# A delta-rule stage whose TensorE order is written by hand: projections ahead of time between the scan's matmuls, the next head's preparation inside the scan

## The chip, the cores and the metric

The kernel runs on one core of a Trainium2 chip. The metric is the device time of one execution in microseconds (us). TensorE (PE in the rows) multiplies matrices, VectorE (DVE), ScalarE (ACT) and GpSimd (POOL) do elementwise work, SyncE (SP) issues the DMA transfers between the chip's main memory and its on-chip memory. Each engine takes its instructions in one fixed order; an instruction waits for its operands, and everything behind it on its engine waits with it. So the order in which a kernel's instructions stand on each engine is part of the program.

## What is computed

One layer with two groups of heads that read the same normalised input through one projection. Group A, eight heads, is a gated delta rule, run once in each direction over chunks of 64 tokens (256 context tokens, then 512 latent tokens):

```
a      = strict_lower(k_beta @ k.T * decay)            # per chunk
t_inv  = solve(eye + a, eye)
u, w   = t_inv @ (v * b), t_inv @ (k_beta * exp(g))
def step(s, chunk):                                    # one chunk after the other
    v_new = u - w @ s
    o     = (q * exp(g)) @ s + intra @ v_new
    s     = s * exp(g_last) + (k * exp(g_last - g)).T @ v_new
```

q, k and v of a head are columns of `h @ w_in`, through a convolution over five tokens and a SiLU. Group B is attention with eight query heads and two key/value heads; its q, k and v are other columns of the same product. Both groups are gated by further columns (z) and go through one output projection. All of it is in float32; the large products are made of three products of a high and a low part each.

## The kernel before, in words

**Projections.** One projection tile makes 128 columns of `h @ w_in` for all tokens: 16 steps over the 2048 inputs, in each three matmuls (high x high, low x high, high x low part; L158) of 512 latent columns, and for k, v and the kv tiles three more of 256 context columns (L160). A k, v or kv tile thus streams 36,864 columns, a q or qa tile 24,576. The weights come by SyncE in four pieces a tile (`wraw`), ScalarE casts the high part (`whi`, L122), VectorE or GpSimd makes the low part (`wlo`, L123). The results stand in the accumulators `pl` (512 columns) and `pc` (256 columns, one buffer), from which ScalarE copies them to a buffer `craw`.

**A head of the delta rule** has three parts. *Post*: VectorE does convolution and SiLU of k, q and v (`gdn_post_k`, `gdn_post_q`, `gdn_post_v`). *Preparation* (`gdn_prep`): transposes to tokens (`t1`, `t2`, `t3`, `tv`), the Gram products q k and k k (`gq` L552, `gc` L557), then the inverse of the triangular blocks. Their 16 x 16 corners go through the main memory to `NE` in another layout, 28 small VectorE operations (L603, L605) solve them, they go back through the memory to `DD`, and TensorE combines the blocks in four groups of tiny matmuls on 32 x 32 tiles (`pxa` L626, `pxb` L632, `pxy` L652 and L662) into `UU`. *Scan* (`gdn_scan`): 12 steps, 4 for the context and 8 for the latent tokens, each doing both directions. A step's chain is: ks (L694, L695: state times k) and, on latent steps, the state times q into `o` (L698, L700); r on VectorE (L703); tr = UU times r (L705); vn on ScalarE (L707); su, two state updates of half the array each (L712), and vn into `o` (L722); the new state st on VectorE (L718, twice). After the last step a head's output is normalised (`on`), transposed (`ot`, L735), scaled by ScalarE (`oc`) and stored to `o_d` (L738).

**The order.** In program order a head's projections stand first, then its preparation, then its scan; after head 7 come four kv tiles and three qa tiles, stored to `kvd` and `qad` for the attention. A scheduler orders all five engines by its own model of times; in this stage nothing is ordered by hand, except that the gates of heads 1 to 7 are issued after a marked instruction of head 0's preparation. So the projections of later heads, the kv and the qa tiles fill TensorE between the scan's matmuls wherever the scheduler put them. The attention, from the transposes of the first kv head on (`kps0`, L877), has a TensorE order written by hand. Its loads are norm weights (`nw`), rotary tables (`rope`, of which VectorE makes `tabk`), the mixer inputs `M` from `o_d`, queries `qc` from `qad` and `kvch` from `kvd`.

Stages in the profiled execution: the input stage and head 0's projections to about 161 us, the delta-rule stage to 860, attention to 1233, output projection to the end.

Of the kernel before, what the change touches and what calls it, by code (L numbers as in the profile page):

```python
# [68 lines left out]
def build(tc, a):  # L69
# [77 lines left out]
    def proj_steps(col, nm, pl, pc=None):  # L147

        for kq in range(4):
            src = w_in[kq * 512:(kq + 1) * 512, col:col + 128].rearrange("(k p) c -> p k c", p=128)  # L150
            hi, lo = wpiece(src, f"{nm}_{kq}", 128)
            for k4 in range(4):
# [8 lines left out]
                yield  # L161
# [177 lines left out]
    for j in range(3):  # L339
        V.tensor_copy(gsb[:, 256 * j:256 * j + 256], gps[32 * j:32 * j + 32])  # L340
    gso = p1a.tile([32, 6, 2, 64], F32, name="gso")
    for lo_c, n in ((0, 4), (4, 8)):
        v = gsb[:, lo_c * 64:(lo_c + n) * 64].rearrange("p (c t) -> p c t", t=64)
        p_lo = 0 if n == 4 else 2
        V.tensor_copy(gso[:, p_lo:p_lo + n // 2, 0], v[:, 0:n // 2])
        V.tensor_copy(gso[:, p_lo:p_lo + n // 2, 1], v[:, n // 2:n][:, ::-1])
    gtp = gtile([128, 6, 32], "gtp")
    for p in range(6):
        T.transpose(out=gtp[:, p], in_=gso[:, p].rearrange("g h t -> g (h t)"), identity=ident[:32, :32])
# [8 lines left out]
    for hf_ in range(2):  # L358
        pr = slice(64 * hf_, 64 * hf_ + 64)
        for v in range(2):  # L360
            d = v if hf_ == 0 else 1 - v
            src = gtp[pr].rearrange("t p (k d h) -> t d k h p", k=2, d=2)[:, d]
            V.tensor_copy(gx[pr, :, :, v], src)
            s2 = adt[pr].rearrange("t k (d h) -> t d k h", d=2)[:, d].unsqueeze(3).to_broadcast([64, 2, 8, 6])
            V.tensor_copy(adv[pr, :, :, v], s2)
# [4 lines left out]
    S.activation(gsc["beta"], flat(gx[:, 0]), AF.Tanh, scale=0.5)  # L370
    V.tensor_scalar(out=gsc["beta"], in0=gsc["beta"], scalar1=0.5, scalar2=0.5, op0=ALU.mult, op1=ALU.add)
# [6 lines left out]
    V.tensor_tensor(out=zg, in0=flat(gx[:, 1]), in1=flat(adv[:, 1]), op=ALU.add)  # L378
    V.tensor_copy(ag, flat(adv[:, 0]))
    V.scalar_tensor_tensor(out=ug, in0=zg, scalar=-1.0, in1=zg, op0=ALU.mult, op1=ALU.min)  # L380
    for q_ in range(0, 96, 12):
        G.tensor_tensor(out=ug[:, q_:q_ + 12], in0=ep[:, q_:q_ + 12], in1=ug[:, q_:q_ + 12], op=ALU.pow)
    es1a.close()

    def gates(h0, h1):
# [18 lines left out]
        gcp = gtile([128, 2, n], "gcp" + nm)  # L404
        gtot = [gtile([128, n], f"gtot{i}" + nm) for i in range(2)]
        gcv = gcp.rearrange("p s (h v q) -> p s h v q", v=2, q=6)
# [12 lines left out]
        V.tensor_scalar(out=gsc["negeg"][:, cols], in0=gsc["negeg"][:, cols], scalar1=-1.0, scalar2=None, op0=ALU.mult)  # L419
        gtr = gtile([n, 128], "gtr" + nm)  # L420
# [7 lines left out]

    gates(0, 1)
# [19 lines left out]

    def gdn_post_k(h, pl, pc):  # L450
        kq = qkp.tile([128, 8, 128], F32, tag="kq", bufs=3, name=f"kq{h}")
        kc = qkp.tile([128, 2, 2, 64], F32, tag="kc", bufs=2, name=f"kc{h}")
# [7 lines left out]
        return kq, kc  # L460

    def gdn_post_q(h, kq, pl):
# [5 lines left out]
    def gdn_post_v(h, pl, pc):  # L468
        vv = qkp.tile([128, 6, 2, 64], F32, tag="vv", bufs=1, name=f"vv{h}")
# [5 lines left out]
        return vv  # L475

    mark = [None]

    def gdn_prep(h, kq, kc, vv):

        nm = f"h{h}"
        UU, IB = UUs[h % 2], IBs[h % 2]
# [11 lines left out]
        for p in range(4):  # L494
            S.activation(jk, t1[:, p], AF.Square, accum_out=ss[:, p:p + 1])
        for p in range(4):
            T.transpose(out=t2[:, p], in_=kq[:, 7 - p], identity=ident)
        S.copy(ktok[64:128, 2:6], t2[64:128])
        for p in range(4):
            S.activation(jk, t2[:, p], AF.Square, accum_out=ss[:, 4 + p:5 + p])  # L500
        t3 = gtile([128, 2, 128], f"t3{nm}")
# [45 lines left out]

        gq = gtile([128, 4, 2, 64], f"gq{nm}")
        for p in range(4):
            for s, c in ((0, p), (1, 7 - p)):  # L550
                kv = kq[:, c].rearrange("p (s t) -> p s t", s=2)
                T.matmul(gq[64 * s:64 * s + 64, p], lhsT=kv[:, s], rhs=kv if s == 0 else kv[:, ::-1],  # L552
                         start=True, stop=True, skip_group_check=True)
        gc = gtile([128, 2, 64], f"gc{nm}")
        for p in range(2):
            for s in range(2):
                T.matmul(gc[64 * s:64 * s + 64, p], lhsT=kc[:, p, s], rhs=kc[:, p, s],  # L557
# [9 lines left out]
        for v in range(2):  # L567
            mul(V, grv[:, v, 2:6], gq[:, :, 0], grv[:, v, 2:6])
            mul(V, grv[:, v, 0:2], gc, grv[:, v, 0:2])
# [7 lines left out]

        vtok = gp.tile([128, 6, 128], F32, tag="vtok", bufs=2, name=f"vtok{nm}")
        for p0_, n in ((0, 2), (2, 4)):
            tv_ = gtile([128, n, 128], f"tv{nm}_{p0_}")  # L580
            for p in range(n):
                T.transpose(out=tv_[:, p], in_=vv[:, p0_ + p].rearrange("c s t -> c (s t)"), identity=ident)
            for p in range(n):
                S.activation(vtok[:, p0_ + p], tv_[:, p], AF.Copy, scale=vin[:, p0_ + p:p0_ + p + 1])
# [12 lines left out]
        mark[0] = V.memset(NE.rearrange("w j i -> w (j i)")[:, 0:256:17], 1.0).ins  # L597
# [12 lines left out]

# [591 lines left out]
```

## Time and profile before

| | |
|---|---|
| median of 3 runs | 1435.78 us (1430.89 to 1436.18) |
| the profiled execution's own time | 1433.8 us |
| its span, first to last instruction | 1432.0 us |
| mean granted TensorE clock | 0.986 |
| TensorE, VectorE, GpSimd, ScalarE busy | 1316.3, 733.7, 500.1, 494.2 us |

Busy time says which engine has the most work, not where the end is set. For that the span is cut into stages, and in each one reads how long TensorE stood and what ended its waits. A wait is printed as "engine, instruction <- what ended it: us in total, times, longest". In the names, h is a head's number left out, `bk` is the bank that holds ks, tr and one of the su, and "64*128" is the part of the array that a matmul uses.

### The profile page before, as it was taken

Reading aid. Unit: us, or ns where it says so; the run is one execution under the profiler, and the core shown is the slowest. Engines: PE = TensorE matmul, PEld = TensorE weight load, DVE = VectorE, ACT = ScalarE, POOL = GpSimd, SP = SyncE. Lnnn points to the kernel's source line nnn. Section 1 sums busy time; section 2 is a strip of 40 time slices with the busy share of each in tenths; the row PEclk is TensorE's granted clock in tenths of the full one; section 3 lists DMA queues with packets and bytes.
Section 4 is the critical chain, followed back from the end, with each engine's and each line's share of the span. In section 5 each row is a group of like instructions: output and inputs, shape, how many; then the busy total and the mean of one; then the engine's idle time right before and its main releaser. Section 6 shows DMA issues by size and latency. Waiting matters only on the chain. (4 is left out here: it accounts for less than half of the span.)

```text
span 1432.0 us, 25185 instructions
## 1 busy us (share of the span) xinstructions
PE 1316.3 (92%) x9710; PEld 1011.0 (71%) x9710; DVE 733.7 (51%) x1618; ACT 494.2 (35%) x1212; POOL 500.1 (35%) x473
## 2 busy tenths in 40 slices
PE   3898899999999999999899996999999999998997
PEld 1455678666677777777677785777787877776785
DVE  3443686757456575656362135535648456533222
ACT  4111354243243433343232223444334433533221
POOL 1011554443424343333323244333343333333530
PEclk9999999999999999999999998999999999999999
DMA  9999444232313131413122277223425243464202
GB/s 308 279 295 283 121 100 101 47 73 43 83 38 96 37 95 31 98 43 82 35 58 62 55 224 223 68 67 104 131 70 160 74 130 103 160 235 139 89 35 98
DMA packets 278708, 163.58 MB, mean 114 GB/s; under 512 B 79868, under 2 KB 252501, under 8 KB 277565
## 3 DMA queue, kind: packets, MB, share of 16 engines
q1 hardware_dynamic: 278589, 161.98, 41.3%
q8 instruction: 76, 1.25, 0.4%
q14 instruction: 43, 0.35, 0.1%
HBM read 150.43 MB, written 11.51 MB: 113 GB/s over the span
## 5 line engine op out<-in xcount | busy, mean ns | idle before, releaser
L123 POOL TENSOR_TENSOR wlo_z<-wraw_z,whi_z 128x512 fp32r<-128x512 f32 x64 | 86.0, 1344 | 152.8 <-ACT whi_z L122 152.8
L686 POOL TENSOR_SCALAR keh<-ktokh,esuf 128x128 f32<-128x128 f32 x88 | 55.3, 629 | 169.7 <-PE bkh L712 169.6
L158 PE MATMUL zl<-hhL,whi_z 128*128 128x512 f32 x256 | 108.4, 423 | 0.0
L158 PE MATMUL zl<-hlL,whi_z 128*128 128x512 f32 x256 | 103.1, 403 | 0.0
L158 PE MATMUL zl<-hhL,wlo_z 128*128 128x512 f32 x256 | 102.9, 402 | 0.0
L707 ACT ACTIVATE vnh<-bkh,cch 128x128 f32<-128x128 f32 x96 | 35.2, 367 | 174.2 <-PE bkh L705 174.1
L140 PE MATMUL po<-wlo_wo,mh 128*128 128x512 f32 x192 | 76.7, 400 | 6.4 <-POOL wlo_wo L123 4.8
L139 PE MATMUL po<-whi_wo,mh 128*128 128x512 f32 x192 | 75.8, 397 | 0.1
L141 PE MATMUL po<-whi_wo,ml 128*128 128x512 f32 x192 | 75.8, 395 | 0.0
L1042 DVE SCALAR_TENSOR_TENSOR gacc<-graw,scol,gacc 128x512 f32<-128x512 f32 x60 | 56.1, 934 | 32.7 <-DMA graw<-in_w_ada 32.2
L123 POOL TENSOR_TENSOR wlo_qa<-wraw_qa,whi_qa 128x512 fp32r<-128x512 f32 x32 | 43.2, 1351 | 73.5 <-ACT whi_qa L122 73.5
L718 DVE SCALAR_TENSOR_TENSOR sth<-sth,egl,suh 128x128 f32<-128x128 f32 x80 | 27.7, 346 | 77.8 <-PE bkh L712 77.2
L123 POOL TENSOR_TENSOR wlo_wo<-wraw_wo,whi_wo 128x512 fp32r<-128x512 f32 x24 | 35.6, 1483 | 82.6 <-ACT whi_wo L122 82.5
L122 ACT CAST whi_z<-wraw_z 128x512 fp32r<-128x512 f32 x64 | 39.6, 621 | 64.8 <-PE zl L158 21.7
L158 PEld LDWEIGHTS zl<-hhL,wlo_z 128*128 128x128 f32 x256 | 49.3, 193 | 11.9
L158 PEld LDWEIGHTS zl<-hlL,whi_z 128*128 128x128 f32 x256 | 49.6, 194 | 8.7
L158 PEld LDWEIGHTS zl<-hhL,whi_z 128*128 128x128 f32 x256 | 49.6, 194 | 8.7
L123 DVE TENSOR_TENSOR wlo_wo<-wraw_wo,whi_wo 128x512 fp32r<-128x512 f32 x24 | 20.0, 838 | 68.7 <-ACT whi_wo L122 66.1
L251 PE MATMUL ada<-wada,cs 128*32 128x256 f32 x512 | 41.9, 414 | 12.6 <-DMA wada<-in_w_ada 12.6
L319 POOL TENSOR_TENSOR wlo<-wraw,whi 128x384 fp32r<-128x384 f32 x16 | 16.0, 1004 | 105.6 <-ACT whi L318 105.6
L123 POOL TENSOR_TENSOR wlo_q<-wraw_q,whi_q 128x512 fp32r<-128x512 f32 x24 | 33.3, 1389 | 54.8 <-ACT whi_q L122 46.6
L703 DVE SCALAR_TENSOR_TENSOR rh<-bkh,negeg,vtokh 128x128 f32<-128x128 f32 x88 | 30.8, 350 | 41.9 <-PE bkh L695 41.4
(387 smaller groups left out, 4099.8 us busy)
## 6 DMA issues: line engine op xcount, KB each, us to landing
wada<-in_w_ada SPq DMA_DIRECT2D x128, 256.0 KB, 5.1
graw<-in_w_ada SPq DMA_DIRECT2D x64, 256.0 KB, 2.7
wraw_z<-in_w_in SPq DMA_DIRECT2D x64, 256.0 KB, 2.8
wraw_wo<-in_w_out SPq DMA_DIRECT2D x48, 256.0 KB, 3.0
wraw_qa<-in_w_in SPq DMA_DIRECT2D x32, 256.0 KB, 2.8
wraw_k<-in_w_in SPq DMA_DIRECT2D x28, 256.0 KB, 2.9
wraw_q<-in_w_in SPq DMA_DIRECT2D x28, 256.0 KB, 2.7
wraw_v<-in_w_in SPq DMA_DIRECT2D x28, 256.0 KB, 2.8
```

The lines of the kernel that those rows point to most:

```text
L122: S.copy(hi, raw)
L123: (lo_eng or G).tensor_tensor(out=lo, in0=raw, in1=hi, op=ALU.subtract)
L139: T.matmul(out, lhsT=lh, rhs=rh, start=start, stop=False, skip_group_check=True)
L140: T.matmul(out, lhsT=lh, rhs=rl, start=False, stop=False, skip_group_check=True)
L141: T.matmul(out, lhsT=ll, rhs=rh, start=False, stop=stop, skip_group_check=True)
L158: T.matmul(pl, lhsT=lw, rhs=rt[0][:, k], start=st, stop=sp, skip_group_check=True)
L251: T.matmul(ada_ps[32 * g:32 * g + 32], lhsT=cs[:, kk], rhs=wt[:, kk % 4].rearrange("p s c -> p (s c)"), start=kk < 4, stop=kk >= KT - 4, s ...
L686: G.tensor_scalar(out=ke, in0=ktok[:, p], scalar1=gsc["esuf"][:, gcol:gcol + 1], scalar2=None, op0=ALU.mult)
L703: V.scalar_tensor_tensor(out=r, in0=ks, scalar=gsc["negeg"][:, gcol:gcol + 1], in1=vtok[:, p], op0=ALU.mult, op1=ALU.add)
L707: S.activation(vn, tr, AF.Copy, scale=cc[:, 0, w:w + 1])
L718: V.scalar_tensor_tensor(out=sn[:, d], in0=st[:, d], scalar=egl[:, half, gcol:gcol + 1], in1=su, op0=ALU.mult, op1=ALU.add)
L1042: V.scalar_tensor_tensor(out=acc, in0=raw, scalar=scol[:, k:k + 1], in1=acc, op0=ALU.mult, op1=ALU.add)
```

## The change

TensorE's order from the end of head 0's projections to the last qa tile is now the program's order (`manual_schedule` for TensorE alone); the other engines are still ordered by the scheduler. The program order is written with generators:

- `feed` runs over the projection tiles in the order q1, k1, v1, kv0, kv1, then k, q, v of heads 2 to 7, then kv2, kv3, qa0, qa1, qa2. `pull(n)` takes steps from it until n columns are streamed.
- `gdn_scan` yields after ks and o (2600 columns are pulled there), after tr (2900) and after su and o (2900): 35 slots a head.
- `gdn_prep` of the next head is cut into 11 pieces. One piece is emitted at each of the slots in `PREP_AT`; `gc` is in the fifth (slot 9), `pxa` in the eighth (slot 24).
- The output transposes of a head (`ot`) are emitted at slot 6 of the next head's scan; those of head 7 after all else.
- VectorE's, ScalarE's and GpSimd's operations of the scan, and those of the gates, get the scheduler's priority `first_of_all` (2500, where the solve's operations have 1500).

Also: `gc` and its use stand behind `gq`'s, and `tv` and `vtok` behind the solve; `kc` has three buffers instead of two, `ke` two instead of three, `r` one instead of two; a kv tile is stored in two transfers; the gates' totals share a bank. The arithmetic and the number of matmuls are the same.

```
+    F1, F2, F3 = 2600, 2900, 2900
+    PREP_AT = (0, 2, 4, 6, 9, 11, 13, 24, 26, 29, 31)
+    def first_of_all():
+        return tc.high_priority(offset=2500)
+    es_p0.enter_context(tc.manual_schedule(engines={mybir.EngineType.PE}))
...
+    def feeding():
+        yield from feed_q(1)
+        yield from feed_k(1)
+        yield from feed_v(1)
+        for i in range(2):
+            yield from feed_kva(i)
+        for h in range(2, NH):
+            yield from feed_k(h)
+            yield from feed_q(h)
+            yield from feed_v(h)
+        for i in range(2, 4):
+            yield from feed_kva(i)
+        for h in range(QSPILL):
+            yield from feed_qa(h)
...
+    def pull(n):
+        debt[0] += n
+        while debt[0] > 0:
+            c = next(feed, None)
+            if c is None:
+                debt[0] = 0
+                return
+            debt[0] -= c
...
+    for n in (3000, 5500, 5500, 4000, 12000, 4000):
+        pull(n)
+        next(prep, None)
+    run(g1, 5000, 9000, 3000)
...
+    run(prep, 4000, 24000, 4000, 5000, 4000)
+    tail = None
+    for h in range(NH):
+        while h + 1 < NH and h + 1 not in fed:
+            pull(1)
+        scan = gdn_scan(h)
+        prep = gdn_prep(h + 1) if h + 1 < NH else iter(())
+        slot = 0
+        for n in scan:
+            if n is None:
+                break
+            pull(n)
+            if slot in PREP_AT:
+                next(prep, None)
+            if slot == 6 and tail is not None:
+                next(tail, None)
+            slot += 1
+        for _ in prep:
+            pull(3000)
+        tail = scan
+    pull(12000)
+    next(tail, None)
+    for _ in feed:
+        pass
```

What this does to the order is shown at three places. First TensorE at the end of the stage. Before, around the output transposes of head 7 (`oth`; `kvl` and `kvx` are the accumulators of tile kv3):

```order
L160 MATMUL kvx_8835<-hlC,whi_kv_0_8838 128x256
L158 MATMUL kvl_8834<-hhL,wlo_kv_0_8839 128x512
L160 MATMUL kvx_8835<-hhC,wlo_kv_0_8839 128x256
L158 MATMUL kvl_8834<-hhL,whi_kv_0_8838 128x512
L160 MATMUL kvx_8835<-hhC,whi_kv_0_8838 128x256
L158 MATMUL kvl_8834<-hlL,whi_kv_0_8838 128x512
L160 MATMUL kvx_8835<-hlC,whi_kv_0_8838 128x256
L158 MATMUL kvl_8834<-hhL,wlo_kv_0_8839 128x512
L735 MATMUL oth_8450<-cmain,onh_8442 128x128 x4
L160 MATMUL kvx_8835<-hhC,wlo_kv_0_8839 128x256
```

After, from the last step of head 7's scan (now L722 to L728 for ks and o, L735 for tr, L755 for vn into o) to the first attention transposes (`kpsh`) and the first z projection:

```order
L722 MATMUL bkh_11_9160<-sth_10_9156,kq_7391 64x128
L723 MATMUL bkh_11_9160<-sth_10_9156,kq_7391 64x128
L726 MATMUL oh_8981<-sth_10_9156,qeh_8076 64x128
L728 MATMUL oh_8981<-sth_10_9156,qeh_8076 64x128
L735 MATMUL bkh_11_9160<-rh_11_9165,UU_2041 128x128
L755 MATMUL oh_8981<-vnh_11_9168,IB_1559 128x128
L770 MATMUL oth_9181<-cmain,onh_9173 128x128 x4
L998 MATMUL kps_9268<-cmain,kvch_9266 128x128 x6
L159 MATMUL zl_9298<-hhL,whi_z_0_9301 128x512
```

The kv and qa tiles that stood around and behind the output transposes are gone from there; in after, the last projection matmul of the feed stands in step 5 of this scan, and steps 6 to 11, oth and kps0 follow one another with no projection between.

Second, SyncE from the store of head 7's output on. Before, from three rows behind that store (`wraw` are weights, `graw` weights of the gate vector):

```order
L816 DMA nw_9230<-in_q_norm_w 128x128
L817 DMA nw_9230<-in_k_norm_w 128x128
L131 DMA wraw_qa1_1_9056<-in_w_in 128x4x128
L785 DMA kvd_8458<-craw0_1530 128x768
L827 DMA ropek0_9237<-in_rope 128x512
L131 DMA wraw_qa1_2_9074<-in_w_in 128x4x128
L827 DMA ropek1_9239<-in_rope 128x512
L1038 DMA graw0_0_10297<-in_w_ada 128x512
L1038 DMA graw0_1_10300<-in_w_ada 128x512
L131 DMA wraw_qa1_3_9092<-in_w_in 128x4x128
L872 DMA kvch00_9261<-kvd_8458 128x768
L872 DMA kvch01_9306<-kvd_8458 128x768
```

After, from the store itself:

```order
L773 DMA o_d_1469<-och7_9172 128x512
L937 DMA nw_9235<-in_q_norm_w 128x128
L938 DMA nw_9235<-in_k_norm_w 128x128
L948 DMA ropek0_9242<-in_rope 128x512
L948 DMA ropek1_9244<-in_rope 128x512
L1172 DMA M0_9207<-o_d_1469 128x512
L1172 DMA M1_9208<-o_d_1469 128x512
L1172 DMA M2_9209<-o_d_1469 128x512
```

Four rows on, behind M3 to M6:

```order
L1172 DMA M7_9214<-o_d_1469 128x512
L1036 DMA qc0_9262<-qad_1563 128x512
L1036 DMA qc1_9264<-qad_1563 128x512
L993 DMA kvch00_9266<-kvd_1562 128x768
L993 DMA kvch01_9311<-kvd_1562 128x768
```

The loads for the attention stand directly behind the store of head 7's output, with the eight M loads ahead of qc and kvch; before, weights of the qa tiles stood between them, and the M loads came later than all of these rows.

Third, TensorE at the first scan matmul of head 0 (L705 before, L735 after). Before (`gq` belongs to the preparation of head 1, `ql` to the projection of head 2):

```order
L158 MATMUL ql_3214<-hhL,wlo_q_1_3236 128x512
L158 MATMUL ql_3214<-hhL,whi_q_1_3235 128x512
L552 MATMUL gqh_2596<-kq_2301 64x128 x3
L705 MATMUL bkh_0_1959<-vtokh_1683,UU_1587 128x128
L552 MATMUL gqh_2596<-kq_2301 64x128 x4
L712 MATMUL suh_0_1963<-vnh_0_1961,keh_0_1957 128x128
L712 MATMUL bkh_0_1959<-vnh_0_1961,keh_0_1957 128x128
L552 MATMUL gqh_2596<-kq_2301 64x128
L158 MATMUL ql_3214<-hlL,whi_q_1_3235 128x512
L158 MATMUL ql_3214<-hhL,wlo_q_1_3236 128x512
```

After (`pxy` belongs to the preparation of head 0, `kvl` and `kvx` to tile kv0, `t1` to the preparation of head 1):

```order
L684 MATMUL pxyh_2306<-DTh_2065,XTh_2287 32x32 x2
L684 MATMUL pxyh_2306<-DDh_2064,XTh_2287 32x32
L735 MATMUL bkh_0_2374<-vtokh_1906,UU_1552 128x128
L159 MATMUL kvl_2152<-hhL,whi_kv_1_2296 128x512
L161 MATMUL kvx_2153<-hhC,whi_kv_1_2296 128x256
L159 MATMUL kvl_2152<-hlL,whi_kv_1_2296 128x512
L161 MATMUL kvx_2153<-hlC,whi_kv_1_2296 128x256
L159 MATMUL kvl_2152<-hhL,wlo_kv_1_2297 128x512
L161 MATMUL kvx_2153<-hhC,wlo_kv_1_2297 128x256
L504 MATMUL t1h_2387<-cmain,kq_1687 128x128 x4
L744 MATMUL suh_0_2398<-vnh_0_2376,keh_0_2372 128x128
L744 MATMUL bkh_0_2374<-vnh_0_2376,keh_0_2372 128x128
```

The scan of head 0 now starts straight behind its own preparation, at a point where the feed has reached kv0; counted over the whole order, about 145,000 projection columns stand ahead of this matmul before and about 114,000 after, and head 2's q and v stand between the scans of head 0 and head 1.

More of the change, by code (lines that the diff above doesn't have):

```diff
@@ L568, in gdn_prep @@
             mul(V, grv[:, v, 2:6], gq[:, :, 0], grv[:, v, 2:6])
+        yield
+        gc = gtile([128, 2, 64], f"gc{nm}")
+        for p in range(2):
+            for s in range(2):
+                T.matmul(gc[64 * s:64 * s + 64, p], lhsT=kc[:, p, s], rhs=kc[:, p, s],
+                         start=True, stop=True, skip_group_check=True)
+        for v in range(2):
             mul(V, grv[:, v, 0:2], gc, grv[:, v, 0:2])
@@ L656, in gdn_prep @@
         V.tensor_copy(XT, pxy[:, 0])
+        yield
         for p in range(6):
@@ new lines, in run @@
+    def run(gen, *pulls):
+        for n in pulls:
+            pull(n)
+            if next(gen, gen) is gen:
+                return
+        for _ in gen:
+            pull(2000)
+    g0, g1 = gates(0, 1), gates(1, NH)
+    pull(1500)
+    with first_of_all():
+        next(g0, None)
+    pull(16000)
+    with first_of_all():
+        next(g0, None)
+    pull(3000)
+    with first_of_all():
+        next(g0, None)
+    prep = gdn_prep(0)
+    for n in (3000, 5500, 5500, 4000, 12000, 4000):
+        pull(n)
+        next(prep, None)
```

239 lines of the change are left out of this document (132 added, 107 removed).

## The prediction

> **What bounds the kernel now.** I read the page first. Its first lines say what the whole span is made of.
>
> ```profile
> span 1432.0 us, 25185 instructions
> PE 1316.3 (92%) x9710; PEld 1011.0 (71%) x9710; DVE 733.7 (51%) x1618; ACT 494.2 (35%) x1212; POOL 500.1 (35%) x473
> ```
>
> TensorE is busy for 92% of the span and no other engine for more than 51%, so the order of TensorE can win at most the time in which TensorE stands, and lose whatever it adds to that. Next I cut the span by stage, with the columns start and end, length, and busy time by engine with the granted clock after POOL's column.
>
> ```profile
> 161.00:251.00 90.00, 82.82 (x730) 67.39 (x729) 67.36 (x179) 42.10 (x117) 48.70 (x35) 0.98 0.38 90
> 251.00:860.00 609.00, 581.53 (x5456) 443.36 (x5453) 327.34 (x853) 205.17 (x568) 224.60 (x247) 0.99 0.29 71
> 860.00:905.00 45.00, 33.74 (x146) 26.91 (x145) 24.71 (x41) 16.33 (x54) 19.94 (x18) 0.81 0.62 189
> ```
>
> The change touches these three stretches: the start (161 to 251, idle 7.2 us), the scans with their fillers (251 to 860, idle 609.0 - 581.5 = 27.5 us) and the entry to attention (860 to 905, idle 11.3 us). The waits of TensorE between 251 and 860 come from another view (total, times, longest), and one row each from the same view for 161 to 251 and for 860 to 905.
>
> ```profile
> PE oth L735 <- DVE onh L732: 7.0, 6, 2.0
> PE pxah L626 <- DVE DTh L619: 4.5, 4, 1.2
> PE pxbh L632 <- issue: 4.2, 4, 1.7
> PE bkh L694 <- DVE sth L718: 2.1, 3, 1.3
> PE oth L735 <- DVE tmh L603: 2.0, 2, 1.0
> PE pxyh L662 <- issue: 1.6, 1, 1.6
> PE ktp L877 <- DVE kn L852: 5.1, 1, 5.1
> ```
>
> No wait is large. The biggest group is the transposes of a head's output (oth), 9.0 us in all; the scan itself (bk) waits for 2.1 us. Last the inside of one scan step, from the timeline of TensorE (start, duration), VectorE and ScalarE, in head 7:
>
> ```profile
> 785.92 0.32 PE L694 MATMUL bkh<-sth,kq 128*64 128x128 f32 x1
> 786.97 0.38 PE L705 MATMUL bkh<-rh,UU 128*128 128x128 f32 x2
> 787.31 0.39 PE L158 MATMUL kvl<-hhL,whi_kv 128*128 128x512 f32 x1
> 787.54 0.28 PE L160 MATMUL kvx<-hhC,whi_kv 128*128 128x256 f32 x1
> 787.97 0.34 PE L712 MATMUL suh<-vnh,keh 64*128 64x128 f32 x1
> 788.95 0.28 PE L160 MATMUL kvx<-hlC,whi_kv 128*128 128x256 f32 x1
> 789.06 0.39 PE L158 MATMUL kvl<-hhL,wlo_kv 128*128 128x512 f32 x1
> 789.38 0.32 PE L694 MATMUL bkh<-sth,kq 128*64 128x128 f32 x1
> 786.41 0.35 DVE L703 SCALAR_TENSOR_TENSOR rh<-bkh,negeg,vtokh 128x128 f32<-128x128 f32 x1 [0.80 <-PE bkh L695]
> 788.46 0.35 DVE L718 SCALAR_TENSOR_TENSOR sth<-sth,egl,suh 128x128 f32<-128x128 f32 x1 [1.70 <-PE bkh L712]
> 788.72 0.34 DVE L718 SCALAR_TENSOR_TENSOR sth<-sth,egl,bkh 128x128 f32<-128x128 f32 x1
> 787.45 0.37 ACT L707 ACTIVATE vnh<-bkh,cch 128x128 f32<-128x128 f32 x1 [2.59 <-PE bkh L705]
> ```
>
> Four numbers come out of this. A 512-column projection matmul occupies TensorE for 787.54 - 787.31 = 0.23 us, so 0.455 ns a column. The same matmul ahead of a small-tile matmul takes 789.38 - 789.06 = 0.32 us, so a change between the full array and a 64-wide tile costs about 0.09 us. The 256 columns at 787.54 need 0.12 us and the change 0.09, yet the state update (su) starts 0.43 us later: 0.2 us of hidden waiting for vn, which no idle row shows. And the whole step takes 3.46 us, with 3072 projection columns in it (1.40 us), so the scan's own matmuls occupy about 1.86 us.
>
> **The change part by part**, against the profiled execution's own time of 1433.8 us (span 1432.0; the median of the runs shown is 1435.8, from 1430.9 to 1436.2, so this execution lies 2 us under the median).
>
> *Array changes.* Counted in the two orders from the gate transposes to the first attention transposes, there are 506 changes between full and small tiles before and 433 after. 73 x 0.094 = 7 us less; nothing hides them, they are TensorE's own time. **-7**; 0 if the shorter streaks drain less.
>
> *The start.* Before the first scan matmul of head 0, before streams about 145,000 projection columns and after about 114,000: 31,000 x 0.455 ns = 14.1 us of work moved behind it. It is a gain only if the scan of head 0 starts 14 us sooner. Its chain is gates, Gram products, the triangular solve on VectorE, and pxa:
>
> ```profile
> 237.22 0.57 DVE L619 STREAM_TRANSPOSE DTh<-DDh 128x384 f32<-128x384 f32 x1
> 240.93 0.22 PE L626 MATMUL pxah<-DTh,grh 32*32 32x32 f32 x2
> 251.30 0.48 PE L705 MATMUL bkh<-vtokh,UU 128*128 128x128 f32 x2
> ```
>
> DT is ready at 237.8 and pxa follows 3.1 us later: by hand that goes. The gates' VectorE work now runs first of all, and nothing else of head 1 is between pxa and the scan; I put 3 us on both, from the 10.4 us that now lie between pxa and the first scan matmul. So the scan starts 6 us sooner for 14.1 us of missing cover: **+8**. Ends: +3 if the chain shrinks by 11 us, +15 if it does not shrink at all and something slips by a microsecond.
>
> *Waits in the scans.* The fixed slots stand 6 or more matmuls of a projection (2304 to 3072 columns, 1.05 to 1.4 us) at each of the three hand-overs of a step. The hand-over from vn to su needs 787.97 - 786.97 = 1.0 us, that to ks 789.38 - 787.97 = 1.4 less its own 0.4, that to tr 1.05. So the scan's waits go, the hidden ones too: 0.2 us in about half of some 90 steps, 10 us, with the visible 27.5 us 37 us together. oth goes to a fixed slot in the next head's scan, long after it is ready; pxb and pxy keep some 6 us, since their waits are for evacuations that are no shorter. What is late next is pxa. One head of before shows its chain:
>
> ```profile
> 493.06 0.45 PE L557 MATMUL gch<-kc 128*64 128x64 f32 x6
> 503.25 0.17 DVE L603 TENSOR_TENSOR tmh<-NEh 96x14 f32<-96x14 f32 x1
> 516.14 0.16 DVE L605 TENSOR_TENSOR NEh<-NEh,tmh 96x14 f32<-96x14 f32 x1
> 526.42 0.22 PE L626 MATMUL pxah<-DTh,grh 32*32 32x32 f32 x2 [1.07 <-DVE DTh L619]
> ```
>
> gch to pxa is 33.4 us; its solve on VectorE took 12.9 us, where 28 operations of about 0.2 us need some 6 with other work between, so I take 31. In the order of after, about 41,500 columns (18.9 us) and five steps (9.3 us) stand between gch and pxa: 28.2 us. So pxa stops TensorE by 0 to 5 us in each of 7 heads; I take 2.5, 17 us. And ten tiles now follow one another on the single context accumulator (v, then k), which must wait for ScalarE's copy; the nearest row is two kv tiles that do so:
>
> ```profile
>   ACT craw L784: 0.6, 2
> L182 ACT COPY craw<-kx x7: 365/374/398, 186.6 to 665.6; 128x256 f32<-128x256 f32 x7
> ```
>
> 0.3 us each, up to 0.8 where a cast is ahead of the copy: 5 us for ten. The spill stores of the kv and qa tiles now pass through SyncE's queue during the scans, ahead of transfers of the solve, and wait there for that same copy; I cost them at nothing, since weights are loaded a tile ahead, and at 0.4 us for each of 7 tiles if not. With 3 us for small slips, these among them, 31 us stay of 37. **-6**, from -26 (pxa never late, no slips) to +12 (5 us a head).
>
> *The end of the stage.* Here the order of after is plain: the feed of projections runs out in step 6 of the last scan. The steps left (5.5) stand bare, then oth of head 7, then kps0 directly. In before, kv3 and three qa tiles, some 100,000 columns or 45 us, stood between. A bare step is its chain, from the rows above: ks to r 0.49, r 0.35, to tr 0.21, to vn 0.48, vn 0.37, to su 0.15, to st 0.49, both st 0.60, together 3.14, with the next ks 3.2 us instead of 1.86 us of own work: 5.5 x 1.34 = +7. The last oh, the transposes and the loads behind them stand in the next rows, with the landing time of the M loads last.
>
> ```profile
> 808.71 0.49 PE L722 MATMUL oh<-vnh,IB 128*128 128x128 f32 x2
> 812.98 0.63 PE L735 MATMUL oth<-cmain,onh 128*128 128x128 f32 x4 [1.09 <-DVE onh L732]
> 815.65 0.46 SPq L738 DMA_DIRECT2D o_d<-och  x1
> 871.60 3.64 SPq L1051 DMA_DIRECT2D M<-o_d  x8
> M<-o_d SPq DMA_DIRECT2D x8, 256.0 KB, 5.1
> 859.88 0.82 PE L877 MATMUL kps<-cmain,kvch 128*128 128x128 f32 x6
> 870.00:880.00 10.00, 3.77 (x15) 2.94 (x16) 5.91 (x9) 3.79 (x11) 4.68 (x4) 0.63 0.90 308
> ```
>
> Last oh to oth is 4.3 us, of which TensorE waited 1.1 and now all: +3. Behind oth, SyncE's queue in after holds the store of o_d, the two norm loads, two rope loads, eight M loads, two qc, and only then kvch, for which kps0 waits. From the rows: oth to the issue of o_d 2.7, o_d with nw and rope issues 2.3 (five at about 0.46), eight M and two qc 4.6, then kvch lands in about 5 behind the 2.5 MB ahead of it, since 3 MB at 308 GB/s last 9.7 us from the first M: 14.7, less oth's own 0.6: 14. Before had all of this under the 45 us of projections (kps0 follows without a wait at 859.88). I take 13, between 6 (kvch bound only by its own issue) and 17. The entry that follows then finds loaded weights and an emptier queue, where ktp waited 5.1 us and the clock fell to 0.63: -4 of its 11.3 us. **+19**, from +9 to +24.
>
> Here a rule speaks against the change. In the row 870 to 880, TensorE is busy for 3.8 of 10 us and its granted clock is 0.63. The Trainium skill, "TensorE: Matmul & The Clock Gate", Part 1: The HAM clock gate, says that a window of about 3.4 us without enough work halves the clock, and that a like window of work restores it; by that, the 13 us wait would end in about 3.4 us at half speed, some 1.7 us more. The drop in the row agrees in direction; no run here shows the window.
>
> Sum: 8 - 7 - 6 + 19 = +14, so 1433.8 + 14 = **1448**.
>
> **The rivals.**
>
> *Faster.* The solve of the next head is done when pxa comes up (31 us becomes 28), and the chain of head 0 is 11 us shorter: +3 - 7 - 26 + 19 = -11, **1423**. For it: the steps between are long, and the scan's VectorE work goes first, so no wait is passed on; the present pxa waits are at most 1.2 us. Against it: pxa comes after a fixed number of columns, not when it is ready.
>
> *No change.* The end costs half, since steps 6 to 11 are partly covered by slips of the feed and kvch is issued before M's bytes fill the engines: loads 6, bare 4, oth 3, entry -4 = +9, and +4 in all, **1438**. For it: SyncE issues a load in 0.46 us, and what is ahead of kvch could be issued while the bare steps run. Against it: SyncE's queue, where all of it stands behind the store of o_d.
>
> *Slower still.* The solve's 28 operations stand in VectorE's queue between the state updates of step 5 and of step 7; if their input lands later than the queue reaches them, the scan stands behind them too. The input came 10.2 us after gch in the rows (493.06 to 503.25); the queue reaches it about 2.3 steps of 5.7 us later, 13 us. If it slips by more than 3 us, each head pays the 3 us more: 7 x 3 = +21, **1469**. It decides from a landing 13 us after gch.
>
> *Clock.* During the bare steps TensorE is busy for 1.86 of 3.2 us. At a clock of 0.63 for 5.5 steps its 10.2 us become 16.2, +6, **1454**. No stretch of the trace has TensorE half busy for so long, so it has little for or against it. The page of the Trainium skill named above speaks of idle and busy windows and does not say where 58% falls.
>
> **How the numbers follow.** Forecast 0.37 (own range 1443 to 1457), faster 0.27 (1416 to 1428), no change 0.20, slower still 0.11, clock 0.05. Half a per cent, 7 us, is about what a measurement of this kernel can tell from no change; faster by more has 0.27, within it 0.20, slower by more 0.37 + 0.11 + 0.05 = 0.53. The range for 8 in 10 goes from 1418, inside the faster case, to 1470, the upper rival.
>
> **What would show it.** Right: in the profile after, the last scan's steps are 3.2 us apart with idle rows behind r and vn, kps0 waits over 10 us for the DMA of kvch, the first scan matmul of head 0 is at 244 to 248, oth has no wait. Wrong: kps0 waits under 5 us (the end is not dear); pxa waits under 5 us in all while head periods fall below those of before (faster); waits of bk for st or r of over 20 us (slower still). A start of head 0's scan before 240 would break the first term.

## The result, and the profile after

The changed kernel takes 1470.0 us (median, 1467.1 to 1470.8) where before takes 1435.1: ratio 1.0245, interval 1.022 to 1.0271. It is slower, as forecast, but by 35 us and not by 14, just outside the range on record (1418 to 1470). The profiled execution took 1469.6, its span 1467.8, 35.8 us over before's span; the sums below are made against that. (Of e2_more_columns two of four executions were disturbed; its time is given by the other two.)

The first lines of the page after:

```profile
span 1467.8 us, 25179 instructions
PE 1310.9 (89%) x9710; PEld 1011.6 (69%) x9710; DVE 725.8 (49%) x1618; ACT 493.4 (34%) x1212; POOL 498.9 (34%) x473
```

TensorE has 5.4 us less to do than before, and stands 41 us longer. Its waits over the whole span, the rows of the changed stage alone:

```profile
PE gcp L414 <- issue: 20.2, 1, 20.2
PE kps L998 <- DMA kvch<-kvd: 15.6, 1, 15.6
...
PE pxah L645 <- DVE DTh L637: 12.4, 6, 4.8
...
PE bkh L722 <- DVE sth L749: 8.3, 6, 1.9
...
PE oth L770 <- DVE onh L766: 3.8, 1, 3.8
...
PE kx L161 <- ACT craw L183: 3.7, 5, 1.1
```

Two single waits stand out, one at the start (gcp, the cumulative gates of head 0) and one at the end (kps0, for kvch). Between the heads little is left: the many waits for oth are gone, and what pxa waits is 12.4 us in all, 4.8 of it in head 0. The windows of the two ends, with the middle between them in the second row (start and end, length, busy time by engine from TensorE on, then granted clock, DMA share and GB/s):

```profile
166.00:192.00 26.00, 5.10 (x22) 3.54 (x20) 13.24 (x39) 4.27 (x9) 20.93 (x10) 0.65 0.16 40
261.00:800.00 539.00, 512.79 (x4869) 400.70 (x4870) 295.27 (x791) 193.10 (x543) 202.80 (x221) 0.99 0.28 66
846.00:875.00 29.00, 25.06 (x138) 16.94 (x136) 6.70 (x21) 4.44 (x10) 6.84 (x8) 0.74 0.15 43
882.00:897.00 15.00, 0.30 (x2) 0.30 (x3) 1.50 (x5) 0.04 (x1) 0.00 (x0) 0.50 0.83 307
```

The middle is dense at a clock of 0.99; at both ends the clock falls, down to 0.50. What holds the start is read from VectorE and GpSimd:

```profile
175.50 0.16 DVE L403 SCALAR_TENSOR_TENSOR ug<-ug,w_g 128x12 f32<-128x12 f32 x1
186.81 1.81 DVE L397 TENSOR_SCALAR s_g<-ug 128x84 f32<-128x84 f32 x1 [11.15 <-POOL ug L386]
191.68 0.17 DVE L407 SCALAR_TENSOR_TENSOR gg__1452<-zg,ag 128x12 f32<-128x12 f32 x1
167.62 19.15 POOL L386 TENSOR_TENSOR ug<-ep,ug 128x12 f32<-128x12 f32 x8 [3.11 <-DVE ug L384]
```

GpSimd raises `ug` to a power in eight pieces, 2.4 us each. Head 0 needs the first piece. The operation on 84 columns is the first gate operation of heads 1 to 7 and needs the seven others; it stands in VectorE's queue ahead of the last seven of head 0's gate operations (those on 12 columns), so these wait 11.15 us with it, and gcp on TensorE behind them. And the end, TensorE's rows from the bare steps (tr of steps 6 to 11) to the attention, and SyncE's:

```profile
855.35 0.49 PE L735 MATMUL bkh<-rh,UU 128*128 128x128 f32 x2 [0.23 <-DVE rh L732]
858.50 0.49 PE L735 MATMUL bkh<-rh,UU 128*128 128x128 f32 x2 [0.23 <-DVE rh L732]
862.09 0.80 PE L735 MATMUL bkh<-rh,UU 128*128 128x128 f32 x2
866.11 0.80 PE L735 MATMUL bkh<-rh,UU 128*128 128x128 f32 x2
870.12 0.79 PE L735 MATMUL bkh<-rh,UU 128*128 128x128 f32 x2
874.13 0.79 PE L735 MATMUL bkh<-rh,UU 128*128 128x128 f32 x2
880.01 1.09 PE L770 MATMUL oth<-cmain,onh 128*128 128x128 f32 x4 [3.78 <-DVE onh L766]
896.70 1.54 PE L998 MATMUL kps<-cmain,kvch 128*128 128x128 f32 x6 [15.60 <-DMA kvch<-kvd]
```

```profile
882.06 0.34 SPq L773 DMA_DIRECT2D o_d<-och  x1
884.43 5.13 SPq L1172 DMA_DIRECT2D M<-o_d  x8
889.94 0.94 SPq L1036 DMA_DIRECT2D qc<-qad  x2
891.25 0.94 SPq L993 DMA_DIRECT2D kvch<-kvd  x2
```

The first two bare steps are 3.15 us apart, the last ones 4.01 us, not 3.2, and their tr takes 0.80 us where it took 0.49 in the first two. Between them the granted clock falls:

```profile
856.00:858.00 2.00, 1.31 (x14) 1.02 (x14) 0.61 (x2) 0.30 (x1) 0.94 (x2) 1.00 0.48 164
858.00:860.00 2.00, 1.16 (x12) 0.74 (x8) 0.35 (x1) 0.37 (x1) 0.00 (x0) 0.94 0.34 99
860.00:862.00 2.00, 2.00 (x13) 1.22 (x10) 0.92 (x3) 0.00 (x0) 0.60 (x1) 0.50 0.00 0
```

### The profile page after: what moved, and what is told of

Its sections match the earlier page's. It is cut to its first block, busy times and chain, and to the rows that moved or that the text cites. A ratio compares the mean times of both kernels' runs of the same rounds, so it can differ in the third digit from the quotient of the medians.

```text
span 1467.8 us, 25179 instructions
## 1 busy us (share of the span) xinstructions
PE 1310.9 (89%) x9710; PEld 1011.6 (69%) x9710; DVE 725.8 (49%) x1618; ACT 493.4 (34%) x1212; POOL 498.9 (34%) x473
## 4 chain that ended last, share of the span: by engine, by line
PE 64%; DVE 12%; DMA 9%; issue 5%; POOL 4%; ACT 3%; SPq 2%; POOLq 0%; DVEq 0%; ACTq 0%
PE zl L159 9%; PE qal L159 5%; PE vl L159 5%; PE kl L159 4%; PE ql L159 4%; PE po L140 3%; PE kvl L159 3%; PE po L141 3%; PE po L139 3%; DMA wada<-in_w_ada 3%; PE vx L161 2%; PE suh L744 2%; DMA graw<-in_w_ada 2%; PE kx L161 2%; PE bkh L722 2%
## 5 line engine op out<-in xcount | busy, mean ns | idle before, releaser
L712 POOL TENSOR_SCALAR keh<-ktokh,esuf 128x128 f32<-128x128 f32 x88 | 61.4, 698 | 66.0 <-PE bkh L744 65.2
L751 DVE SCALAR_TENSOR_TENSOR sth<-sth,egl,suh 128x128 f32<-128x128 f32 x80 | 27.5, 344 | 84.8 <-PE bkh L744 82.0
L1163 DVE SCALAR_TENSOR_TENSOR gacc<-graw,scol,gacc 128x512 f32<-128x512 f32 x60 | 53.0, 884 | 19.5 <-DMA graw<-in_w_ada 19.2
L159 PE MATMUL qal<-hhL,whi_qa 128*128 128x512 f32 x128 | 54.1, 423 | 0.0
L159 PE MATMUL kl<-hhL,whi_k 128*128 128x512 f32 x112 | 52.7, 470 | 0.0
```

The costliest lines, as they stand in the source:

```text
L159: T.matmul(pl, lhsT=lw, rhs=rt[0][:, k], start=st, stop=sp, skip_group_check=True)
L712: G.tensor_scalar(out=ke, in0=ktok[:, p], scalar1=gsc["esuf"][:, gcol:gcol + 1], scalar2=None, op0=ALU.mult)
L1163: V.scalar_tensor_tensor(out=acc, in0=raw, scalar=scol[:, k:k + 1], in1=acc, op0=ALU.mult, op1=ALU.add)
```

## The experiments

Twelve kernels, each compared with before on the chip that it ran on. "The start" is the time of head 0's first scan matmul (251.3 before, 261.1 after).

**e1_gates_behind: the mark put back.**

```
-        V.memset(NE.rearrange("w j i -> w (j i)")[:, 0:256:17], 1.0)
+        mark[0] = V.memset(NE.rearrange("w j i -> w (j i)")[:, 0:256:17], 1.0).ins
...
+            with tc.issue_after(mark[0]):
+                done = next(gen, gen) is gen
...
-    g0, g1 = gates(0, 1), gates(1, NH)
+    g0, g1 = gates(0, 1), behind_mark(gates(1, NH))
```

> The changed kernel with one thing put back: VectorE's gate operations of heads 1 to 7 are again issued behind head 0's NE memset. Theory 1 (the start was lost in VectorE's queue): the operation on 84 columns that waited 11.15 us for GpSimd's power operations no longer stands in front of head 0's gates, so gcp comes at 179 to 182 us instead of 191.9, TensorE's wait there is 8 to 10 us instead of 20.2, the first scan matmul of head 0 comes at 249 to 252 instead of 261.1, and the time falls from 1470 by 10 to 12 to about 1459. Rival (TensorE's own order is the loss: gcp stands too early in it, and the chain behind is as long anyway): the first scan matmul stays after 257 and the time falls by less than 4.

1457.5 us, ratio 1.0173 (1.0144 to 1.0201), 12.6 less than after. gcp came at 178.2, the start at 251.1. Its waits of TensorE between 161 and 251:

```profile
PE gcp L414 <- issue: 8.4, 1, 8.4
PE gcp L414 <- DVE gg__1452 L407: 8.2, 1, 8.2
```

The mark is worth about 12 us (12.6 by the medians, 10 by the two ratios, whose intervals are 4 us to either side), and theory 1 holds for that part. It isn't the whole: the start is back where before has it, but TensorE still stands 16.6 us on the way (at head 0's gcp and at that of heads 1 to 7), where before streamed projections.

**e5_before_unmarked: the same part of the change, done to before alone.**

```
-            with tc.issue_after(mark[0]):
-                gates(1, NH)
+            gates(1, NH)
```

> The kernel before with one part of the change done to it: the gates of heads 1 to 7 are no longer issued behind the mark. Their first operation on 84 columns then stands in VectorE's queue ahead of 7 of head 0's gate operations, as in the changed kernel. Theory 1 (that operation holds head 0's chain whatever orders TensorE): VectorE stands about 11 us before it, gcp comes at 188 to 192 instead of 178.0, the first scan matmul of head 0 at 259 to 264 instead of 251.3; since the scheduler fills TensorE with projections meanwhile, not all of it is lost: +3 to +10. Rival (it is harmless where TensorE is not ordered by hand): within 2 us of before.

1457.2 us, ratio 1.0161 (1.0126 to 1.0197): 23 us slower than before, more than twice what I expected at most, and the start at 269.7. VectorE, ScalarE and TensorE in this run:

```profile
186.59 1.81 DVE L393 TENSOR_SCALAR s_g<-ug 128x84 f32<-128x84 f32 x1 [13.39 <-POOL ug L382]
190.25 0.59 ACT L185 COPY craw<-vlat 128x512 f32<-128x512 f32 x1 [16.10 <-DVE ug L399]
191.77 0.58 PE L160 MATMUL kx<-hhC,whi_k 128*128 128x256 f32 x1 [19.71 <-ACT craw L182]
```

The scheduler did put projections there, but they stood too: VectorE holds ScalarE, whose copy of the context accumulator TensorE's next k tile waits for. The start is 18.4 us later than before's (of the rest of its profiled span, 2.8 us lie in the scans and 1.7 behind kps0), so the operation on 84 columns costs no less without the hand order than with it. What I had assumed, that a scheduler fills the gap, did not hold here, where the fillers need the engine that stands.

**e2_more_columns: the pull ahead of gcp raised, VectorE as in after.**

```
-    pull(16000)
+    pull(58000)
```

> The changed kernel with 58000 instead of 16000 projection columns pulled ahead of gcp, VectorE as it is. Theory 1 (20.2 us of TensorE stand uncovered, while head 0's chain sets when the scan starts): the wait at gcp falls from 20.2 to 0 to 3 us, the first scan matmul of head 0 stays at 258 to 264, and 42000 columns (19 us) less are left for later; since the feed then ends some 5 steps earlier in the last scan, which stand bare at about 2 us more each, the time falls by 6 to 10, to about 1462. Rival (the convolutions of head 1 come earlier with the projections and lengthen head 0's chain on VectorE): the first scan matmul comes after 266 and the time does not fall.

Ratio 1.0128 (1.0091 to 1.0165), about 1452: 18 us less than after, more than expected. The gcp wait is gone, but the start comes at 268.4, since the projections now wait for VectorE themselves (9.4 us for a low part of the k weights). That much of the rival is true. The gain comes out all the same, because those columns no longer stand between scan 0 and scan 1, where the loop pulls whatever head 2 still lacks; the feed ends in the same step of the last scan as in after, so no further step is bare. I had overlooked that.

**e6_start_filled: e1, and both gaps filled.**

```
-    pull(16000)
+    pull(32000)
...
-    run(g1, 5000, 9000, 3000)
+    run(g1, 23000, 9000, 3000)
```

> The kernel of e1_gates_behind (1457) with the pulls ahead of the two gcp raised from 16000 and 5000 to 32000 and 23000 columns; 146,700 columns now stand ahead of head 0's scan, as many as in before. Theory 1 (the start costs what stands uncovered): the waits at the two gcp fall from 16.6 to under 4 us, the first scan matmul of head 0 stays at 250 to 254, the clock between 161 and 251 stays over 0.95, and the time falls by 11 to 15 to about 1444. Rival (more columns ahead delay the chain by as much): the first scan matmul comes after 260 and the time falls by less than 5.

1446.5 us, ratio 1.0088 (1.0058 to 1.0119), 11 less than e1. The start comes at 248.4, and the window of the start reads as before's did (82.8 us busy), at a clock of 1.00:

```profile
161.00:251.00 90.00, 82.76 (x741) 68.33 (x741) 63.57 (x171) 35.86 (x91) 46.44 (x34) 1.00 0.38 92
```

So the start of the changed kernel cost about 23 us (23.5 by the medians, 22.5 by the ratios): about half by the missing mark, half by too few columns ahead of the two gcp.

**e3_z_first: 40 steps of the z tiles moved ahead of kps0.**

```
+        fill(40)
         for kv in range(2):
             kns = k_norm(kv)
```

> The changed kernel with 40 projection steps of the first z tiles (28 us of TensorE at full clock) ahead of the first attention transposes in TensorE's order; 16 of them come to stand in the bare steps of head 7's scan, 22 between its output transposes and kps0. Theory 1 (the bare steps and the uncovered loads cost the end of the stage 28 us): the steps 6 to 11 of the last scan take 3.2 to 3.6 us instead of 4.01, the wait of kps0 for kvch falls from 15.6 to under 3 us, and the time falls by 15 to 20 to about 1452, the attention paying some us at its end, where those z steps are missing. Rival (the end is paid anyway, since the same TensorE work is only moved, and the attention's end stands as long as the stage's end did): the time falls by less than 5.

1467.0 us, ratio 1.0231 (1.0198 to 1.0264), 3 less than after, with intervals that overlap. The steps took 3.48 to 3.74 us and kps0 waited 3.1, as theory 1 says; yet the rival is right about the time. The same stretch of the attention, 200 to 380 us behind kps0, in this kernel and in after:

```profile
1099.10:1279.10 180.00, 158.54 (x801) 128.98 (x800) 107.60 (x177) 70.78 (x148) 49.12 (x37) 0.94 0.36 105
```

```profile
1096.70:1276.70 180.00, 172.80 (x888) 140.91 (x887) 107.99 (x172) 74.53 (x158) 61.27 (x46) 0.99 0.40 115
```

14 us more of TensorE stand idle there, at a lower clock. From kps0 to the end it is 569.7 us where after has 571.1, with 28 us less work. So the attention here needs its fillers, and the end of the stage has to be covered by work of its own.

**e4_unused_matmuls and e12_few_unused: matmuls that nothing reads, in the bare end.** `idle_work(n)` issues n matmuls of 512 columns. e4 is after with

```
             if c is None:
                 debt[0] = 0
+                idle_work(min(n // 512, 3))
                 return
...
-    pull(12000)
+    idle_work(16)
     next(tail, None)
-    for _ in feed:
-        pass
+    idle_work(50)
```

and e12 is e6 with one matmul in place of three (`idle_work(1)`).

> The changed kernel with matmuls added whose result nothing reads: three of 512 columns at each of the three hand-overs of the bare steps, 16 ahead of the output transposes of head 7 and 50 ahead of kps0. They add work and remove none. Theory 1 (half of the loss in a bare step is the clock, which TensorE's 58% share lets fall): the granted clock between 846 and 897 us rises from 0.5 to 0.74 to over 0.95, the steps 6 to 11 take 3.3 to 3.6 us instead of 4.01, and the time falls by 2 to 5, to about 1466. Rival (the step's chain of hand-overs is 4 us long at any clock, the prediction's 3.2 was too short): the steps stay at 3.9 to 4.2 us and the time stays or rises by up to 2.

> The kernel of e6_start_filled (1446.5) with matmuls added whose result nothing reads: one of 512 columns at each hand-over of the bare steps (in e4_unused_matmuls it was three, which alone filled 3.94 us a step), 17 ahead of head 7's output transposes and 50 ahead of kps0. Theory (a bare step's chain is 3.2 us at full clock, and 4.01 us is what the clock of 0.5 makes of it): the granted clock stays over 0.95 from the first bare step to kps0, the last steps take 3.1 to 3.5 us, and what follows kps0 starts at full clock; the time falls by 3 to 7, to about 1442. Rival (the chain is 4 us long by itself): the steps stay at 3.9 us or more and the time does not fall.

e4: 1471.1 us, ratio 1.0252 (1.0219 to 1.0285), no change. The clock was 1.00, but the steps took 3.94 us: nine matmuls of 0.23 us and the step's own 1.86 are 3.96, so I had filled the step beyond its chain, and the time told nothing. e12: the steps took 3.14, 3.15, 3.15, 3.14, 3.14 us, where e6 has 3.14, 3.50, 4.01, 4.01, 4.01. The windows of the last scan in e12, and in e6:

```profile
828.00:850.00 22.00, 20.08 (x133) 13.29 (x131) 5.74 (x18) 3.83 (x9) 4.98 (x6) 1.00 0.17 48
```

```profile
830.00:850.00 20.00, 16.13 (x90) 10.76 (x90) 5.13 (x16) 2.76 (x7) 3.07 (x4) 0.63 0.09 30
```

The chain of a bare step is 3.14 us and the rest was the clock; that is shown. The time, 1443.6 and ratio 1.0076 (1.0049 to 1.0104), is 2.9 us under e6, as much as the steps save, but the intervals overlap.

**e7_end_kept: the feed made to last.**

```
-    F1, F2, F3 = 2600, 2900, 2900
+    F1, F2, F3 = 2300, 2500, 2500
...
-        for i in range(2):
-            yield from feed_kva(i)
         for h in range(2, NH):
...
-        for i in range(2, 4):
+        for i in range(4):
             yield from feed_kva(i)
```

> The changed kernel with its start as it is, and the feed so set that it lasts: kv0 and kv1 come behind head 7's v, and 2300, 2500 and 2500 columns are pulled instead of 2600, 2900, 2900. 18,000 columns then stand between the last scan step and head 7's output transposes and 38,400 between these and kps0, and no scan step is bare. Theory 1 (bare steps, oth and the loads cost the end some 30 us, and the smaller pulls still cover the scan's hand-overs): kps0 waits under 2 us, oth under 1 us, steps of the last scan stay under 5.5 us at a clock of 1.0, and the time falls by 22 to 30, to about 1444. Rival (the smaller pulls bring the scan's and the solve's waits back): waits of bk and pxa between heads 0 and 7 rise from 22 to over 35 us and the time falls by less than 15.

1475.4 us, ratio 1.0289 (1.0253 to 1.0325): 5 us over after, with intervals that overlap. Both ends of the expectation came true at once. oth and kps0 wait for nothing, and the rival takes the gain and more:

```profile
PE pxah L645 <- DVE DTh L637: 42.9, 6, 9.3
```

With 36,000 columns instead of 41,000 between gc and pxa, and shorter steps, TensorE stands at pxa for 7 us on average, up to 9.3, in six of seven heads, until the solve is done.

**e8_both: the start of e6 and the end of e7.**

> Both together: the start of e6_start_filled and the end of e7_end_kept. Theory 1 (start and end are separate losses on the path, and the rest of the hand order gains some 19 us over before): the two gains add up to 34 to 42 us, 1430 to 1436 with the start's gain of 26, and if the steady gain is as the trace of the changed kernel shows it, as low as 1418: I expect 1424. Rival (the two share a cause, since the projections are the same ones and can stand in one place only): the gains add up to less than 25, and the time stays over 1445.

1453.2 us, ratio 1.0131 (1.0098 to 1.0163), 7 over e6, though the intervals overlap: the gains don't add up, but not for the rival's reason. oth and kps0 wait for nothing, while pxa waits 24.5 us and gc 8.3.

**e9_pxa_later: e8 with the solve given more room.**

```
-    PREP_AT = (0, 2, 4, 6, 9, 11, 13, 24, 26, 29, 31)
+    PREP_AT = (0, 1, 3, 4, 6, 8, 10, 26, 28, 31, 33)
```

> The kernel of e8_both (1453) with other slots for the next head's preparation: gc at slot 6 instead of 9 and pxa at slot 26 instead of 24, so that about 49,000 instead of 36,000 columns and 6.7 instead of 5 steps stand between them. Theory 2 (the smaller pulls that keep the end covered uncovered the solve: its chain from gc to pxa is about 33 us whatever stands beside it, and e8_both waits 24.5 us at pxa and 8.3 at gc): the waits at pxa fall under 5 us in all and the time by 20 to 28, to about 1429, under before's 1434. Rival (the solve's operations stand in VectorE's queue behind scan operations of fixed steps, so the chain stretches with the slots): pxa still waits over 15 us, and the time falls by less than 10.

1428.5 us, ratio 0.9961 (0.9939 to 0.9983), 25 less than e8. The waits at gc and pxa in this run:

```profile
PE gch L584 <- DVE grh L212: 8.5, 7, 2.4
...
PE pxah L646 <- DVE DTh L638: 3.7, 2, 1.9
```

Theory 2 holds: where the solve is covered, the end that e7 covers pays.

**e10_kvch_first: e6 with the M loads behind kvch.**

```
-    for i in range(8):
-        SY.dma_start(M[i], o_d[i])
...
             v_split(kv, fill)
+            if kv == 0:
+                for i in range(8):
+                    SY.dma_start(M[i], o_d[i])
```

> The kernel of e6_start_filled (1446.5) with seven of the eight M loads issued behind the first two kvch loads instead of ahead of them; the end stands bare as in the changed kernel. Theory (kps0's wait is the issue of the loads in SyncE's queue and their bytes): kvch is issued some 3.5 us sooner and has about 1 MB ahead of it instead of 2.5 MB, the wait of kps0 falls from 15.4 to 8 to 11 us, and the time falls by 4 to 7, to about 1441. Rival (kvch waits for the table that VectorE makes of the rope loads, and its issue does not come sooner): the wait stays over 13 us.

1443.0 us, ratio 1.0054 (1.0033 to 1.0075), 3.5 under e6 with intervals that overlap; kps0 waits 12.0 us instead of 15.4, between what theory and rival expected. SyncE:

```profile
861.70 0.43 SPq L1198 DMA_DIRECT2D M<-o_d  x1
865.57 1.13 SPq L1002 DMA_DIRECT2D kvch<-kvd  x2
```

and VectorE:

```profile
864.85 1.50 DVE L212 TENSOR_TENSOR tabk<-ropek,nw 128x512 f32<-128x512 f32 x5 [8.59 <-DMA ropek<-in_rope]
```

In the queue kvch stood behind one M load, but it was issued 3.9 us after that, 7.1 us after o_d where e6 has 9.0: it is loaded into the buffers of the rope loads, and VectorE read these for the table from 864.85 on. So taking the M loads away wins 3.4 us of the wait and no more, since the rival's path, the rope loads and the table, stands right behind the queue; in e10 the 12 us that are left are that path, from oth over the store of o_d, the rope loads and the table to the landing of kvch.

**e11_more_pulled: e9 with 100 columns more at each hand-over.**

```
-    F1, F2, F3 = 2300, 2500, 2500
+    F1, F2, F3 = 2400, 2600, 2600
```

> The kernel of e9_pxa_later with 2400, 2600 and 2600 columns pulled instead of 2300, 2500, 2500; 30,700 instead of 38,400 columns are left between head 7's output transposes and kps0 (14 us instead of 17.5, about what the loads need). Theory 2: the solve is covered by 1 us more a head, kps0 waits under 2 us, and the time is within 4 of e9_pxa_later, about 1428. Rival (the end is covered to the microsecond only): kps0 waits 3 to 5 us and the time is that much over e9_pxa_later.

1424.4 us, ratio 0.9932 (0.9907 to 0.9957): the fastest of all, 10 us under before, and 4 under e9, where the intervals overlap. kps0 waits 0.9 us. Its start (252.3) and its way from kps0 to the end (572.1) are those of before (251.3 and 572.1), and as many columns stand ahead of its first scan as in before. So the 12.0 us by which its profiled span is shorter (it was the fastest of its six executions) are all won between, in the scans. That stretch, from head 0's first scan matmul to kps0, in before and in e11:

```profile
251.30:859.90 608.60, 581.13 (x5450) 443.13 (x5450) 327.07 (x852) 204.87 (x568) 224.20 (x247) 0.99 0.29 71
```

```profile
252.30:847.90 595.60, 564.32 (x5456) 434.89 (x5456) 307.85 (x842) 209.57 (x590) 229.41 (x247) 0.99 0.28 68
```

TensorE is busy for 16.8 us less with as many matmuls, and its visible waits grow by 3.8 us, from 27.5 to 31.3.

## Why the prediction was wrong

The profiled executions lie 35.8 us apart and the forecast said 14. Of the 22 us between, 16 are the start and 8 the end; the scans gave 2 back.

**The start, +8 forecast, about +24 measured: the step that failed.** The scan of head 0 came 9.8 us later than before, not 6 sooner, with the same 14.1 us of work missing: 24 us. I wrote that the gates' VectorE work "now runs first of all" and took 3 us off for it and for the shorter way from pxa to the scan; +15 was the far end, "if it does not shrink at all". The diff also removes `issue_after` for the gates of heads 1 to 7, which my section on the change does not list, and I costed that line at nothing: their first operation came to stand ahead of the last seven of head 0's, behind 19 us of GpSimd. e1 (about 12 us) and e5 (23 us on before) show it; e6 shows the other half, columns missing ahead of a wait that TensorE can't pass in a fixed order.

**Array changes and waits in the scans, -7 and -6 forecast.** After the start (+24) and the end (below, +27) the difference of the spans, 35.8, leaves -15 for both. e11 has both without start and end, with slots and pulls of its own: -12. The size was about right, and so was its kind: I had counted 10 us of hidden waits and 7 of array changes, both inside the busy time, as gone and some 3.5 us of visible waits as added, and e11 has 16.8 less busy and 3.8 more idle. How the 16.8 divide into array changes and hidden waits no run shows. The waits themselves were others than forecast: in after pxa waited 7.6 us behind head 0 instead of 17, and ks of a scan's second step waited 8.3 us in six heads for the first state (L749), which I had not listed. VectorE's rows ahead of one of these waits (`on` is the normalised output of the head before, `cacc_v` a convolution):

```profile
516.18 0.69 DVE L766 TENSOR_TENSOR onh<-oh,msh 128x512 f32<-128x512 f32 x1 [2.39 <-POOL msh L206]
516.78 1.01 DVE L195 SCALAR_TENSOR_TENSOR cacc_v<-craw,cvT,cacc_v 128x770 f32<-128x770 f32 x1
517.71 0.28 DVE L749 COPY sth<-suh 128x128 f32<-128x128 f32 x1
```

The state is copied only behind an operation that waits 2.39 us for GpSimd. It is so in five of the six heads (1.7 to 2.4 us); in head 0 the operation ahead of the copy belongs to the next preparation and waits 2.14 us for a load.

**The end, +19 forecast, about +27 measured.** oth: 2.7 us more idle, +3 forecast. The loads: 15.6, 13 forecast. In after SyncE's queue sets the issue of kvch, as I had said, but its eight M loads took 5.13 us to issue and not 3.64; close behind the queue stand the rope loads and the table (e10). The bare steps: six and not 5.5, and from tr to tr they took 3.15, 3.59, 4.02, 4.01 and 4.01 us, 9.5 over 1.86 each, about +10 instead of +7. Their chain is 3.14 us, as summed, but the clock made 4.01 of it from the third step on. I had this as a rival of its own at 0.05, with a price of 6 us; it is a part of the forecast case, at about 3 us (e12). It is the clock gate of the Trainium skill, "TensorE: Matmul & The Clock Gate", Part 1: The HAM clock gate, which halves the clock after an idle window of about 3.4 us. The trace agrees in the half clock: some 5 us behind the last projection it went from 1.00 to 0.50. But TensorE had no gap of more than 0.61 us in those 5 us and was about 60% busy, and the page does not say up to which busy share a window counts as idle. The entry behind kps0 gained 1 us, -4 forecast.

**The rivals.** "Slower still" had the price, 1469, by luck: no scan stood behind the solve, and all waits of bk for st or r came to 13.2 us, where that case needed over 20. What came of its mechanism are the 8.3 us above, behind other operations of VectorE's queue. "Faster" put -33 on the scans, where -15 and -12 were measured; that e11 lands at 1424, next to its 1423, says nothing for it, since e11 pays for neither start nor end and that case had +3 and +19 there. That the end would be half as dear was wrong.

## What to carry to other kernels

When one engine's order is written by hand, its fillers have to be counted up to each wait and behind the last one; where they ran out here, the clock went too. A line that only keeps an instruction behind another in a queue (here `issue_after`) has a price of its own; before it is removed, look what its instructions wait for and who stands behind them. A cover that is moved to fill one gap opens another: raise the distance of the longest chain (here gc to pxa) together with it.

## What the runs showed of the hardware

A TensorE that was about 60% busy, with gaps of 0.2 to 0.6 us, lost half its clock within some 5 us, and one 512-column matmul more at each of a step's three gaps, read by nobody, kept it at 1.00 (e12). GpSimd's power operation on 128x12 elements took 2.4 us (eight in 19.15), where VectorE's simple operations of that size took 0.17. One VectorE operation that waited 13.39 us for GpSimd held ScalarE's next accumulator copy for 16.10 us and TensorE for 19.71 (e5).
